# Other places for the half stores of a matmul with rotary embedding in ScalarE's program

## The chip, the cores and the metric

The kernel runs on one core of a Trainium2 chip. The metric is the device time of one execution in microseconds (us), as the median of several runs. A profile of one execution is at hand, with its trace.

Words used below: TensorE (PE in the profile) multiplies, VectorE (DVE) and ScalarE (ACT) read its results from PSUM, GpSimd (POOL) adds, SyncE (SP) issues loads. A line that ends in q (ACTq, SPq) is an issue of a DMA on that engine's queue.

## The reference

```python
y = np.matmul(x, weight)                       # x [16, 512, 768], weight [768, 768], float32
y = y.reshape(batch, seq, n_heads, head_dim)   # 12 heads of 64
y1, y2 = y[..., :32], y[..., 32:]
out1 = y1 * cos1 - y2 * sin1
out2 = y2 * cos2 + y1 * sin2
out = np.concatenate([out1, out2], axis=-1).reshape(batch, seq, hidden)
```

The 8192 rows of x are multiplied by one weight matrix, and each head of the result is rotated by tables that depend on the position in the sequence.

## The kernel before, in words

**Tiles, groups, pairs.** The rows make 64 tiles of 128 rows, numbered i. Four tiles make a group g (0 to 15); group g holds four batches at one of four position offsets, so that it needs one row of the tables. A group has two pairs, of two tiles each. A pair is plain or a block pair (the dictionary BLOCKS, L140 to L147). Twelve pairs are block pairs: the second pairs of groups 3 to 13 and of group 15. The other 40 tiles are plain.

**A plain tile.** SP loads it as float32 (`load`, 384 KB, ten buffers xs). ScalarE casts it to float16 (`castx`, xc<-xs). TensorE transposes it into PSUM (`turn_rows`, pt<-ident,xc, twelve half-height transposes that fill both pt banks). ScalarE copies it out (xt<-pt). The next tile's transposes need both banks again, so they wait for this copy. TensorE then multiplies it with the weights (py<-w_sb,xt).

**A block pair.** Both tiles are loaded in four quarters (`load_quarter`) that are arranged so that VectorE's 32x32 transpose finishes the job (xp). Seven pairs are loaded by SP as float32 (three buffers xb, quarters of 192 KB) and cast by ScalarE (`cast_pair`, xd<-xb, 1.6 us each). Five (groups 4, 6, 8, 10 and 12) are loaded by GpSimd with a cast on the way (xh, 96 KB each).

**After the product.** VectorE multiplies PSUM with the cos and sin tables (`rope`, L423), and GpSimd adds the two products into a group's output buffer (ov, L449), half a group (1536 columns) at a time up to group 11, in smaller pieces after that. There are four output buffers, so a group's sums wait for the stores of the group four before it. A store moves half a group, 768 KB (`store`, L481).

**Order of the work.** Every engine executes its program in the order in which the Python code emits it, and waits on semaphores in that order. The main loop (L686 to L724) runs over tiles i from 4 on. In one turn it emits: TensorE's matmuls of tile i (`both`), among them the transposes of a later plain tile and ScalarE's copy of it (`turns`, three tiles ahead); VectorE's transposes of block pairs (`bturns`); a further copy; ScalarE's casts of tiles five ahead or so, at most one in an even turn and two in an odd one (`casts`), and with each cast the load that may use the freed buffer (`pump`); GpSimd's loads; and last the stores that the dictionary `stores` has for this i (L718, L719).

Loads are issued by SP in a list made beforehand (`fetch`). Each load waits until the fifth load before it has landed, and until its buffer has been cast.

**Where the stores stand.** L651 to L664 fill `stores`. For each group but the last, and for its first half (h = 0) and second half (h = 2), it names the turn i in which the store is emitted, and the queue: ScalarE's up to group 12, SP's for groups 13 and 14. A store on ScalarE's queue waits for GpSimd's sum, and what stands behind it in ScalarE's program waits with it. A store that is emitted behind a cast cannot be issued before that cast's load has landed. The last group is stored in pieces at the end.

Between them ScalarE's casts and copies go in tile order. In the middle of the kernel a group has two casts and two copies of plain tiles, and, in every second group, the cast of a block pair between the two copies.

Of the kernel before, what the change touches and what calls it, by code (L numbers as in the profile page):

```python
# [108 lines left out]
def kernel(  # L109
# [23 lines left out]
    QB = 4  # L133
# [3 lines left out]
    LAST = NG - 1  # L137
# [514 lines left out]
    for g in range(LAST):  # L652
        for h in (0, 2):
            i = QB * (g + 1) + h
            q = (g, h * H, (h + 2) * H, "act")
            if g < 3:
                i += g + 1
            elif g < LAST - 4:
                i += QB + (1 if g in (3, LAST - 5) else 2)
            elif g < LAST - 2:  # L660
                i = QB * (LAST - 2) + 2 * (g - LAST + 4) + h // 2
            else:
                q = q[:3] + ("sp",)
            stores.setdefault(i, []).append(q)  # L664
# [21 lines left out]
    for i in range(QB, NTILE):  # L686
        g, s = divmod(i, QB)
# [81 lines left out]
```

## Time and profile before

| | |
|---|---|
| runs, median (lowest to highest) | 151.53 us (151.34 to 152.36), 3 runs |
| the profiled execution's own time | 151.91 us |
| its span, first to last instruction | 150.1 us |
| busy: TensorE, VectorE, ScalarE, GpSimd | 140.4, 127.8, 75.4, 124.0 us |
| DMA: moved, mean rate | 51.27 MB, 342 GB/s |
| ScalarE's half stores, issue to landing | 26, median 9.0 us |
| loads xs, issue to landing | 40, median 9.6 us |
| mean granted TensorE clock | 0.992 |

A row of the timeline has the start in us, the time in us, the engine, the line, the operation with its output and input tiles, and in brackets the idle time before it and what ended that. A row of a DMA queue has the number of packets, the MB and the time that its packets took as a share of 16 DMA engines; the shares of several queues can add to more than 100%. Queue q10 holds ScalarE's stores, q1 SP's loads (and SP's few stores at the end), q0 GpSimd's loads.

### The profile page before, as it was taken

What the parts mean: (1) busy time and instruction counts of PE and PEld (TensorE: products, weight loads), DVE (VectorE), ACT (ScalarE), POOL (GpSimd) and SP (SyncE); (2) the same over time, 40 slices, a digit from 0 to 9 for tenths busy, and PEclk for the clock granted to TensorE, in tenths of its full rate; (3) what the DMA queues carried; (4) which work ended last, traced back from release to release, by engine and by line L of the source; (5) the groups of instructions that cost most, each with busy time, mean ns of one, the idle gap of its engine ahead of it and who ended that gap; (6) DMA issues with size and microseconds to landing.
All of it is one profiled execution on the core that took longest, in us unless ns stands there. A gap on an engine that the chain in (4) does not pass through costs nothing.

```text
span 150.1 us, 4344 instructions
## 1 busy us (share of the span) xinstructions
PE 140.4 (94%) x1900; PEld 115.4 (77%) x1900; DVE 127.8 (85%) x101; ACT 75.4 (50%) x87; POOL 124.0 (83%) x77
## 2 busy tenths in 40 slices
PE   6769999999999999999999999999999996999970
PEld 2335578888888879999999999999999995765850
DVE  0334999888989998999989998999899996999990
ACT  3444798785443655375263734292536547930000
POOL 2000399999999999999999999598999997699990
PEclk9999999999999999999999999999999999999996
DMA  4999999999999999999999999999999999997574
GB/s 133 331 384 403 404 400 269 313 308 329 341 347 391 289 327 293 378 345 254 347 375 378 341 342 358 367 402 331 395 376 402 389 412 411 412 405 316 221 295 147
DMA packets 29155, 51.27 MB, mean 342 GB/s; under 512 B 7248, under 2 KB 15184, under 8 KB 29136
## 3 DMA queue, kind: packets, MB, share of 16 engines
q1 hardware_dynamic: 16336, 28.05, 55.0%
q10 hardware_dynamic: 7360, 20.97, 35.6%
q0 software_dynamic: 5440, 1.97, 11.2%
q8 instruction: 15, 0.25, 0.6%
q14 instruction: 4, 0.03, 0.1%
HBM read 27.79 MB, written 25.17 MB: 353 GB/s over the span
## 4 chain that ended last, share of the span: by engine, by line
DMA 74%; DVE 12%; SPq 6%; ACT 3%; issue 3%; DVEq 0%
DMA xs<-in_x_dram 51%; DMA xb<-in_x_dram 22%; DVE tq L423 8%; DVE w_raw L423 2%; SPq L236 2%; SPq L214 2%; ACT xd L194 1%; ACT xc L194 1%; ACT xt L194 1%; SPq L229 1%; DVE ov L449 1%; DVE xs L423 1%; SPq L501 0%; SPq L503 0%; SPq L534 0%
## 5 line engine op out<-in xcount | busy, mean ns | idle before, releaser
L449 POOL TENSOR_TENSOR ov<-tq 128x512 f32<-128x512 f32 (+3 forms) x35 | 76.7, 2221 | 20.8 <-DVE tq L423 20.6
L423 DVE TENSOR_TENSOR tq<-py,csn 128x1024 f32<-128x1024 f32 (+2 forms) x51 | 74.3, 1494 | 3.9 <-PE py L366 3.0
L366 PE MATMUL py<-w_sb,xt 64*128 64x512 f16 (+1 forms) x768 | 74.4, 323 | 0.0
L366 PEld LDWEIGHTS py<-w_sb,xt 64*128 64x128 f16 x768 | 55.7, 94 | 8.6 <-DVE tq L423 0.7
L366 PE MATMUL py<-w_sb,xp 64*128 64x256 f16 (+1 forms) x528 | 52.6, 323 | 0.0
L194 ACT COPY xt<-pt 128x768 f16<-128x768 f16 x38 | 30.4, 801 | 34.6 <-PE pt L275 30.5
L194 ACT CAST xc<-xs 128x768 f16<-128x768 f32 x40 | 36.0, 907 | 22.3 <-DMA xs<-in_x_dram 22.3
L366 PEld LDWEIGHTS py<-w_sb,xp 64*128 64x128 f16 x528 | 39.7, 94 | 4.3
L423 DVE TENSOR_TENSOR w_raw<-py,csn 128x1024 f32<-128x1024 f32 (+1 forms) x22 | 35.3, 1603 | 2.8 <-PE py L366 2.4
L449 POOL TENSOR_TENSOR ov<-w_raw 128x1536 f32<-128x1536 f32 (+2 forms) x15 | 35.4, 2380 | 0.5 <-DVE w_raw L423 0.4
L341 PE MATMUL py<-w_sb,xt 128*128 128x256 f16 (+1 forms) x102 | 17.0, 317 | 1.4 <-DVE w_sb L194 1.3
L275 PEld LDWEIGHTS pt<-ident,xc 64*128 64x128 f16 x408 | 13.4, 94 | 2.7 <-ACT xt L194 1.6
L275 PE MATMUL pt<-ident,xc 64*128 64x64 f16 x408 | 14.1, 190 | 1.3 <-ACT xt L194 1.3
L341 PEld LDWEIGHTS py<-w_sb,xt 128*128 128x128 f16 x102 | 9.2, 98 | 7.5 <-DVE w_sb L194 2.8
L194 ACT CAST xd<-xb 128x1536 f16<-128x1536 f32 x7 | 11.4, 1633 | 2.6 <-DMA xb<-in_x_dram 2.6
L229 POOL DMA_DIRECT2D xh<-in_x_dram x20 | 11.7, 590 | 0.0
L303 DVE STREAM_TRANSPOSE xp<-xd 128x768 f32<-128x768 f32 x7 | 6.8, 970 | 1.4 <-ACT xd L194 1.4
L194 DVE CAST w_sb<-w_raw 128x768 f16<-128x768 f32 x6 | 3.4, 558 | 4.2 <-DMA w_raw<-in_weight_dram 4.2
L303 DVE STREAM_TRANSPOSE xp<-xh 128x768 f32<-128x768 f32 x5 | 6.2, 1235 | 0.0
L558 PE MATMUL py<-cold 128*128 128x512 f16 x12 | 4.3, 519 | 1.4 <-DVE cold L486 1.4
L194 ACT COPY ov<-py 128x256 f32<-128x256 f32 x1 | 0.4, 372 | 10.1 <-POOL ov L449 10.1
L194 DVE COPY xt<-pt 128x768 f16<-128x768 f16 x2 | 1.1, 558 | 4.9 <-PE pt L260 4.9
(23 smaller groups left out, 22.6 us busy)
## 6 DMA issues: line engine op xcount, KB each, us to landing
out_dram<-ov ACTq DMA_DIRECT2D x26, 768.0 KB, 9.0
xs<-in_x_dram SPq DMA_DIRECT2D x40, 384.0 KB, 9.6
xb<-in_x_dram SPq DMA_DIRECT2D x28, 192.0 KB, 8.9
out_dram<-ov SPq DMA_DIRECT2D x4, 768.0 KB, 4.8
w_raw<-in_weight_dram SPq DMA_DIRECT2D x6, 384.0 KB, 7.5
xh<-in_x_dram POOLq DMA_DIRECT2D x20, 96.0 KB, 8.0
out_dram<-ov SPq DMA_DIRECT2D x1, 384.0 KB, 3.7
out_dram<-ov ACTq DMA_DIRECT2D x1, 384.0 KB, 3.4
```

What stands on the lines that cost most here:

```text
L194: eng.copy(out=o, in_=i_) if e == "act" else eng.tensor_copy(out=o, in_=i_)
L214: do(e, lambda eng: eng.dma_start(out=xs_b[k], in_=x[b].rearrange("(p r) h -> r p h", r=SB)[r]), writes=[f"xs{k}"], dma=f"xs{k}")
L229: do(e, lambda eng: eng.dma_start(out=dst[ts(q, R)], in_=src[r, q]), writes=[f"{name}q{q}"], dma=name)
L236: do(e, lambda eng: eng.dma_start(out=w_raw[:, t, h], in_=wv[t, h]), writes=[f"wr{t}{h}"], dma=f"ov{t}_{1536 * (1 - h)}")
L275: do("pe", lambda eng: eng.transpose(pts[r][:, t, h, :], src[rows, t, h, :], ident[rows, rows]), reads=[f"xc{c}", "ident"], writes=[f"pt{r ...
L303: do("dve", lambda eng: eng.transpose(out=dst, in_=src), reads=rd, writes=[f"xp{z}"])
L341: do("pe", lambda eng: eng.matmul(ps, get(t, h), w_sb[:, t, h, a - s * H : z - s * H], start=start, stop=stop), reads=[key, f"w{t}{h}"], w ...
L366: do("pe", lambda eng: eng.matmul(py[:, a:z], get(t, h)[rows], w_sb[rows, t, h, a - s * H : z - s * H], start=start, stop=not opens and en ...
L423: do("dve", lambda eng: eng.tensor_tensor(out=tq.rearrange("p j (h d) -> p j h d", d=D), in0=ps.rearrange("p (h d) -> p h d", d=D) .unsque ...
L449: do(adder, lambda eng: eng.tensor_tensor(out=ov_b[o][:, ds(c0, w)].rearrange("p (h t d) -> p h t d", t=2, d=HD), in0=tq[:, 0].rearrange(" ...
L558: do("pe", lambda eng: eng.matmul(py[:, ts(b, 512)], cold[:, 0:P], cold, start=True, stop=warmed[0] < WARM - 6), reads=["cold"], writes=[f ...
```

## The change

Only the turns i in which ScalarE's stores up to group 12 are emitted are changed. SP's stores of groups 13 and 14, and everything else, stand as before. TensorE's, VectorE's, GpSimd's and SP's programs are the same; in ScalarE's program the same 26 half stores stand at other places.

```diff
-            if g < 3:
-                i += g + 1
-            elif g < LAST - 4:
-                i += QB + (1 if g in (3, LAST - 5) else 2)
-            elif g < LAST - 2:
-                i = QB * (LAST - 2) + 2 * (g - LAST + 4) + h // 2
+            if g < LAST - 2:
+                i = (((5, 7), (9, 12), (15, 16))[g] if g < 3 else (QB * g + 6, QB * g + 9))[h // 2]
             else:
                 q = q[:3] + ("sp",)
```

Here QB is 4, LAST is 15, and before these lines i is 4 (g + 1) + h. The turns that come of it, for the first and the second half of a group:

| group | before | after |
|---|---|---|
| 0 | 5, 7 | 5, 7 |
| 1 | 10, 12 | 9, 12 |
| 2 | 15, 17 | 15, 16 |
| 3 | 21, 23 | 18, 21 |
| 4 to 9 | 4g + 10, 4g + 12 | 4g + 6, 4g + 9 |
| 10 | 49, 51 | 46, 49 |
| 11 | 52, 53 | 50, 53 |
| 12 | 54, 55 | 54, 57 |

In ScalarE's program this puts a store behind each copy of a plain pair. Around the stores of group 8 the program reads as follows, in order. Before: copy 45, store of group 8's first half, cast 48, cast 49, store of its second half, copy 48, copy 49, store of group 9's first half. After: copy 41, store of group 8's first half, cast 44, cast 45, copy 44, cast of a block pair, store of group 8's second half, copy 45, store of group 9's first half, cast 48, cast 49, copy 48, store of group 9's second half, copy 49, store of group 10's first half. Where a pair's cast stands between two copies (groups with an odd number, 3 to 13), the store that follows it stands behind that cast.

## The prediction

> **What bounds the kernel now.** I read the page first, then TensorE's timeline, ScalarE's timeline, GpSimd's timeline, and the DMA view over short stretches. On the page, TensorE and the DMA engines are both full nearly to the end, and the chain of waits is 74% DMA:
>
> ```profile
> PE 140.4 (94%) x1900; PEld 115.4 (77%) x1900; DVE 127.8 (85%) x101; ACT 75.4 (50%) x87; POOL 124.0 (83%) x77
> ...
> PE   6769999999999999999999999999999996999970
> ...
> DMA  4999999999999999999999999999999999997574
> ...
> DMA 74%; DVE 12%; SPq 6%; ACT 3%; issue 3%; DVEq 0%
> ```
>
> TensorE's timeline decides what can be won. In the table of stretches it is busy without a gap from 18 to 124 us. The only gap after that and before its last instruction at 145.4 is this one:
>
> ```profile
> 123.82 2.11 PE L366 MATMUL py<-w_sb,xp 64*128 64x512 f16 x24
> 127.23 0.35 PE L275 MATMUL pt<-ident,xc 64*128 64x64 f16 x12 [1.29 <-ACT xt L194]
> ```
>
> Its cause stands in ScalarE's timeline. The cast of the last block pair (xd<-xb) waits for its DMA until 124.89, the copy of tile 57 (xt<-pt, 126.37) stands behind that cast, and TensorE's transposes of tile 58 need the PSUM banks that this copy reads:
>
> ```profile
> 122.61 0.91 ACT L194 CAST xc<-xs 128x768 f16<-128x768 f32 x1
> 124.89 1.59 ACT L194 CAST xd<-xb 128x1536 f16<-128x1536 f32 x1 [1.37 <-DMA xb<-in_x_dram]
> 126.37 0.80 ACT L194 COPY xt<-pt 128x768 f16<-128x768 f16 x1
> ```
>
> So at most 1.3 us can be won. What can be lost depends on the loads' slack, smallest at tile 49, whose cast waits for its load until 103.55:
>
> ```profile
> 103.55 0.91 ACT L194 CAST xc<-xs 128x768 f16<-128x768 f32 x1 [2.24 <-DMA xs<-in_x_dram]
> 103.56 0.43 ACTq L481 DMA_DIRECT2D out_dram<-ov  x1
> 105.61 0.80 ACT L194 COPY xt<-pt 128x768 f16<-128x768 f16 x1 [1.15 <-PE pt L275]
> 107.73 0.80 ACT L194 COPY xt<-pt 128x768 f16<-128x768 f16 x1 [1.32 <-PE pt L275]
> ```
>
> TensorE's transposes of tile 49 begin at 107.25. A later load pushes cast 49 (0.91) and behind it the copy of tile 48 (0.80), which frees the banks; the slack is 107.25 - 103.55 - 0.91 - 0.80 = 2.0 us. The second line matters too: the store (second half of group 8) issues just as the load lands, because it stands behind that cast. In the kernel before, second halves of groups 4 to 8 wait behind a late load and so give way to it.
>
> The DMA view shows ScalarE's store ring (q10) beside the loads (q1) and GpSimd's casting loads (q0), first over 67.6 to 71.2, then over 71.2 to 113, then over 118 to 130:
>
> ```profile
> q1 hardware_dynamic: 473, 0.68, 71.0%
> q0 software_dynamic: 647, 0.23, 53.9%
> q10 hardware_dynamic: 1, 0.00, 0.0%
> ```
>
> ```profile
> q10 hardware_dynamic: 2982, 8.64, 53.2%
> q1 hardware_dynamic: 4395, 6.05, 44.3%
> q0 software_dynamic: 1238, 0.45, 8.6%
> ```
>
> ```profile
> DMA packets 1931, 4.92 MB, mean 410 GB/s; under 512 B 138, under 2 KB 399, under 8 KB 1930
> ...
> q10 hardware_dynamic: 1176, 3.41, 70.8%
> q1 hardware_dynamic: 754, 1.50, 32.1%
> ```
>
> Where the store ring is empty the loads have 71% of the engines; where it is full, 44% and less. By the packet records the ring is empty from 50.8 to 53.3, 58.9 to 59.9 and 67.6 to 71.2, and then full, but for 0.3 us, to 135.8.
>
> **The change part by part.** No instruction, byte or buffer is added; stores move in ScalarE's program alone.
>
> Issue times. In the new order a store issues when TensorE hands over the transposes of the copy before it. From those copies: group 2's second half 50.41 to 47.3 (behind tile 21's cast); group 3's 56.72 to 50.5 and 58.84 to 56.7; first halves of groups 4 to 9 some 8 us sooner (group 8: 99.59 to 91.4), second halves 3 to 6 us (103.56 to 97.5); group 10 107.7 and 113.8 for 113.77 and 115.89; group 11 115.9 for 118.19, its second half unchanged.
>
> Their own wait, for GpSimd's sum. Behind a waiting store stand the next copy and casts, and TensorE waits for these. Group 10's first sum ends at 101.06 + 3.46 = 104.5, and its store now issues at 107.7: 3.2 us to spare. The other moved stores have 2.8 us or more, group 1's first half 1.2 (sum done 30.9, copy at 32.05). Cost 0; it would show if GpSimd fell 1.2 to 3 us behind. An issue takes 0.4 us of the sequencer before and after.
>
> Buffers. GpSimd's sums wait for stores four groups back; these have landed some 9 us before they are needed (group 4's first at 76.1, group 8's sum starts at 85.2), so sooner brings nothing: 0.
>
> Price of a half store: 786,432 bytes at the 410 GB/s of 118 to 130 is 1.92 us of all engines.
>
> How far the stores run ahead. The holes at 51, 59 and 68 us get filled. At 103.5 the ring before has finished group 7 and a quarter of group 8's first half (102.65 to 106.54). After, group 8's second half issues at 97.5, starts 3 us later (the row at 99.59 starts at 102.65), takes 4 us, and is three quarters done: 1.5 half stores ahead, 2.9 us of all engines. At 44.3% of the engines the loads are then 2.9 / 0.443 = 6.5 us late. The slack is 2.0, so 4.5 us are missing at tile 49.
>
> What TensorE waits. While it waits, sums and stores stop too and the loads get all engines, 1 / 0.443 = 2.26 us of progress per us: 4.5 / 2.26 = 2.0 us. It comes in pieces of up to 1 us from tile 25 on (slack 1.8), since each wait moves all later needs. Bounds: 0, if filling the holes is free, and 4.5, if the stores in flight keep their share all the while. I take 2.0: in the new ring a store starts 3 us after its issue and finds the one before it all but done, so it soon runs dry.
>
> [...] The row is 2,982 packets of q10 beside 4,395 of q1, the latter partly 768-byte ones, and 53 to 44% in time. [...]
>
> The gap at 127.2. At 124.86, when the last pair lands now, the ring has served half of group 11's first half (123.12 to 126.56); after, with everything 2.0 us later, it has served 0.8 to 1.0 of it, and the next store waits behind tile 58's cast as before. 0.3 to 0.5 half stores more is 0.6 to 1.0 us; I take 0.8. The pair lands at 125.7 and TensorE resumes at 128.0. Being 2.0 late it gets there at 125.94 + 2.0 = 127.9: of the gap of 1.29 only 0.1 is left, and what follows is 0.8 us later.
>
> Group 12's second half moves back, 128.33 to 131.9. It is done by 140 either way, the last store lands at 148.9, and the ring stands idle from 135.8 to 144.5, which is its cover: 0.
>
> Sum: +2.0 - 1.2 = +0.8 us. The profiled execution took 151.91 us (span 150.1 and 1.8 around it), 0.38 above the median 151.53. So 152.7 for it, 152.3 for the median.
>
> **Rivals.**
> Loads starve deeper: the backlog of stores keeps its share while TensorE waits. For it: stores no longer stand behind late casts, and one is nearly always in service. Against: the new ring is limited by its issues from about 100 us on. Wait 2.8 (from where it decides) to 4.5, less the gap of 1.29: +1.5 to +3.2, some 154.0.
>
> The holes are free (the other side). For it: at 50.8 to 53.3 and 67.6 to 71.2 the engines moved only 228 and 255 GB/s. If a store raised that to 410, (410 - 245) x 6.1 us is 1.0 MB or 1.3 half stores for nothing; the lead left is 0.2 stores, 0.9 us of load time, under the slack of 2.0. The last pair lands over 1 us sooner and the gap closes: -1.3, 150.2. It decides once 1.0 half stores are free (the 0.5 left are 2.2 us, about the slack). Against: the queues' shares there add to 125% and 154%, so engines were taken, by small packets.
>
> The clock. TensorE's granted clock is 1.00 in the stretch with the 1.29 us gap, and 0.53 over 147.5 to 150, some 2.1 us after its last instruction. A single wait beyond 2.1 us could therefore halve it; first matmuls at 1.40 and the full clock on record from 4.28 put the loss at half of 2.9, 1.4 us each time. One drop on top of 2.8 us of waiting: +2.9, 154.4. Against: the waits should come in pieces under 1 us. [...]
>
> No effect: the ring serves the stores in the old rhythm, 151.5.
>
> **How the numbers follow.** Forecast 0.48, starving deeper 0.33, free holes 0.10, clock 0.06, no effect 0.03. Faster by over 1% (under 150.0, about what a measurement of this kernel can tell from no change) needs more than the whole gap: half of the free holes' chance, 0.05. Slower by over 1% (over 153.05): deeper starving, the clock and 0.04 of the forecast's upper end, 0.43. The rest, 0.52, is within. Forecast's own range 151.5 to 153.2. The range runs from the free holes, rounded up for a part of them, 150.4, to the wait of 4.5: 151.53 + 3.2, with 0.3 for the 0.38 between executions, 155.0.
>
> **What would show it.** Right: store issues right after copies, no ScalarE wait for GpSimd in the middle; q10 busy at 51 to 53 and 68 to 71; casts waiting longer for xs and xb between 70 and 105; TensorE gaps summing to 2 us there, released by ScalarE casts or copies; the gap near 127 nearly gone. Wrong: no TensorE gap before 120, or one store wait on GpSimd that holds a copy, or gaps over 2 us at one place.

## The result and the profile after

| | kernel before | changed kernel |
|---|---|---|
| runs on the same chip, median (lowest to highest), us | 151.95 (149.65 to 155.84), 22 runs | 153.05 (151.38 to 155.74), 22 runs |
| ratio of the times, with its 95% interval | 1 | 1.0135 [1.0098, 1.0171] |
| a profiled execution's own time (span), us | 151.91 (150.1) | 153.1 (151.2) |
| a second profiled execution (run e1 below) | 150.38 (148.6) | |

Executions more than 1.5% above the fastest of their kernel (11 of the 22 before, 5 of the 22 after) are left out of the ratios but not of the medians, which are 0.7% apart; by that rule e5 has no ratio, and as its profile and those of e2 and e3 are of such executions, no size of a difference is rested on them.

The change made the kernel 1.35% slower, about 2.0 us of 151. The page of the changed kernel has the same busy times, but the chain of waits names other things. Of 74% DMA in the profile before, 17% is left, and TensorE stands first:

```profile
PE 141.4 (93%) x1900; PEld 112.8 (75%) x1900; DVE 128.1 (85%) x101; ACT 75.4 (50%) x87; POOL 124.1 (82%) x77
...
PE 54%; DMA 17%; DVE 14%; issue 3%; SPq 3%; POOL 2%; ACT 2%; ACTq 0%; DVEq 0%; POOLq 0%
```

That is no gain: the shares tell through which instructions one path from the end runs, not whether it became shorter. What TensorE lost is told by its timeline. From 18 us to its last matmul it now has two gaps (stretches without a matmul). First the one in the middle:

```profile
101.64 0.38 PE L366 MATMUL py<-w_sb,xt 64*128 64x512 f16 x1
102.81 3.51 PE L366 MATMUL py<-w_sb,xt 64*128 64x512 f16 x40 [0.79 <-ACT xt L194]
```

and then the one near the end, over a shorter window of the same timeline:

```profile
128.15 0.35 PE L275 MATMUL pt<-ident,xc 64*128 64x64 f16 x12 [1.18 <-ACT xt L194]
```

Together they are 0.79 + 1.18 = 1.97 us, which is 1.3% of 151. Both are of one execution. The second one stands where the profile before had 1.29 us. ScalarE's timeline of the changed kernel gives the cause of the first:

```profile
96.85 0.91 ACT L194 CAST xc<-xs 128x768 f16<-128x768 f32 x1 [3.84 <-DMA xs<-in_x_dram]
97.67 0.79 ACT L194 COPY xt<-pt 128x768 f16<-128x768 f16 x1
100.35 1.61 ACT L194 CAST xd<-xb 128x1536 f16<-128x1536 f32 x1 [1.88 <-DMA xb<-in_x_dram]
100.35 0.90 ACTq L481 DMA_DIRECT2D out_dram<-ov  x2
101.85 0.81 ACT L194 COPY xt<-pt 128x768 f16<-128x768 f16 x1
```

The cast of group 11's block pair (xd<-xb) waits 1.88 us for its load. Tile 45's copy stands behind it and runs at 101.85; TensorE's matmuls of tile 45 resume at 102.81. The store line carries two issues: the second half of group 8 and the first half of group 9 both waited behind that cast. In the kernel before the same stretch has no wait of the pair's cast, because its load landed at 95.89 and not at 100.32:

```profile
97.46 0.80 ACT L194 COPY xt<-pt 128x768 f16<-128x768 f16 x1 [2.09 <-PE pt L275]
98.16 1.66 ACT L194 CAST xd<-xb 128x1536 f16<-128x1536 f32 x1
99.59 0.38 ACTq L481 DMA_DIRECT2D out_dram<-ov  x1
99.69 0.82 ACT L194 COPY xt<-pt 128x768 f16<-128x768 f16 x1
```

The list of ScalarE's waits sums this up (us in total, times, longest). After:

```profile
ACT xc L194 <- DMA xs<-in_x_dram: 32.7, 16, 4.1
ACT xd L194 <- DMA xb<-in_x_dram: 4.4, 4, 1.9
```

Before:

```profile
ACT xc L194 <- DMA xs<-in_x_dram: 22.3, 14, 3.4
ACT xd L194 <- DMA xb<-in_x_dram: 2.6, 2, 1.4
```

Most of the 10.4 us more on the first line are hidden: those casts run ahead of what TensorE needs. In e1, the same program as before, the first line has 15.8 us, so single executions differ here too. The DMA view of the changed kernel shows where the loads' time went. Over 50.8 to 53.3 us, where the store ring was empty before:

```profile
DMA packets 545, 0.89 MB, mean 355 GB/s; under 512 B 209, under 2 KB 304, under 8 KB 545
...
q10 hardware_dynamic: 205, 0.62, 63.7%
q1 hardware_dynamic: 144, 0.19, 24.7%
```

The stores took this hole, and the loads' share fell (before: 50.3%). The engines moved 355 GB/s there instead of 228. But GpSimd's casting loads (q0) also had fewer packets in it, 196 for 697, so a part of that rise is small packets that came at another time. Over 71.2 to 113 the shares are about those of before:

```profile
q10 hardware_dynamic: 2809, 8.14, 50.2%
q1 hardware_dynamic: 4311, 6.10, 44.4%
```

The packet records give the stores' lead. Half stores served (q10), and MB moved by all other queues, nearly all of it loads, up to a time:

| up to, us | 60 | 75 | 90 | 103.5 | 124.9 |
|---|---|---|---|---|---|
| half stores: before | 6.00 | 9.09 | 12.82 | 16.08 | 22.48 |
| half stores: e1, the same program | 6.04 | 9.27 | 12.81 | 16.26 | 22.35 |
| half stores: after | 7.00 | 10.55 | 14.04 | 17.75 | 22.95 |
| loads, MB: before | 15.06 | 17.58 | 20.05 | 22.43 | 25.78 |
| loads, MB: e1 | 15.07 | 17.66 | 20.23 | 22.60 | 25.98 |
| loads, MB: after | 14.77 | 17.17 | 19.74 | 21.73 | 25.37 |

At 103.5 us the stores lead those of the first profile by 1.67 half stores (1.31 MB), and the loads are behind by 0.70 MB. Against e1 the lead is 1.49 (1.17 MB) and the loads are behind by 0.87 MB.

Two kernels further below, e10 and e12, also run the program of the kernel before until past 106 us, where their first moved store stands. So four executions of one program can be set beside the changed kernel at 103.5 us:

| | before | e1 | e10 | e12 | after |
|---|---|---|---|---|---|
| half stores served | 16.08 | 16.26 | 16.62 | 16.81 | 17.75 |
| loads moved, MB | 22.43 | 22.60 | 22.76 | 21.84 | 21.73 |
| all queues, MB | 35.08 | 35.39 | 35.83 | 35.05 | 35.70 |
| group 11's pair landed at, us | 95.89 | 95.31 | 94.39 | 99.19 | 100.32 |

The stores' lead is clear of this spread, with 0.94 half stores against e12, and so is the pair's landing, by 1.1 us (100.50 in e7 and 100.54 in e9, which have the same stores of groups 4 to 9). What all engines moved is not: the 0.61 MB that the lead exceeds the loads' deficit by (0.30 against e1) is no more than executions of one program differ by.

### The profile page after: what moved, and what is told of

The parts are those of the page before. It is cut to its first block, busy times and chain, and to the rows that moved or that the text cites. A ratio compares the mean times of both kernels' runs of the same rounds, so it can differ in the third digit from the quotient of the medians.

```text
span 151.2 us, 4345 instructions
## 1 busy us (share of the span) xinstructions
PE 141.4 (93%) x1900; PEld 112.8 (75%) x1900; DVE 128.1 (85%) x101; ACT 75.4 (50%) x87; POOL 124.1 (82%) x77
## 3 DMA queue, kind: packets, MB, share of 16 engines
q0 software_dynamic: 5440, 1.97, 10.9%
## 4 chain that ended last, share of the span: by engine, by line
PE 54%; DMA 17%; DVE 14%; issue 3%; SPq 3%; POOL 2%; ACT 2%; ACTq 0%; DVEq 0%; POOLq 0%
PE py L366 46%; DVE tq L423 10%; DMA xb<-in_x_dram 7%; DMA xs<-in_x_dram 6%; DMA w_raw<-in_weight_dram 5%; PE py L341 4%; PE pt L275 3%; DVE w_raw L423 2%; POOL ov L449 2%; SPq L214 2%; ACT xd L194 1%; SPq L229 1%; DVE xp L303 1%; PE pt L260 1%; DVE ov L449 1%
## 5 line engine op out<-in xcount | busy, mean ns | idle before, releaser
L366 PEld LDWEIGHTS py<-w_sb,xt 64*128 64x128 f16 x768 | 53.8, 94 | 11.5 <-DVE tq L423 1.5
L366 PEld LDWEIGHTS py<-w_sb,xp 64*128 64x128 f16 x528 | 38.5, 94 | 5.3
L558 PE MATMUL py<-cold 128*128 128x512 f16 x12 | 4.8, 568 | 1.4 <-DVE cold L486 1.4
```

Of the source, the lines that this page charges most:

```text
L366: do("pe", lambda eng: eng.matmul(py[:, a:z], get(t, h)[rows], w_sb[rows, t, h, a - s * H : z - s * H], start=start, stop=not opens and en ...
L558: do("pe", lambda eng: eng.matmul(py[:, ts(b, 512)], cold[:, 0:P], cold, start=True, stop=warmed[0] < WARM - 6), reads=["cold"], writes=[f ...
```

## The experiments

The theory is that of the prediction: bytes of stores that go out sooner take the shared DMA engines from the loads, and TensorE loses only what the lateness has beyond the slack. Rival A, the lost brake: it is the second halves alone, which no longer stand behind a late cast. Rival B, the program: it is the places of the stores in ScalarE's program, whatever bytes they carry. Rival C, the window: SP has too few loads in flight (`AHEAD`, each load waits for the fifth before it) to catch up.

All runs are kernels with the turns as a table, `i = PLACES[g][h // 2]`, one pair (first half, second half) per group 0 to 12; the diffs show the rows that differ. Each ratio is against the kernel before in the same session.

**e1: the kernel before, once more**

```diff
-                i = (((5, 7), (9, 12), (15, 16))[g] if g < 3 else (QB * g + 6, QB * g + 9))[h // 2]
+                i = PLACES[g][h // 2]
+    PLACES = ((5, 7), (10, 12), (15, 17), (21, 23), (26, 28), (30, 32), (34, 36), (38, 40), (42, 44), (46, 48), (49, 51), (52, 53), (54, 55))
```

> The kernel before once more, with the places of the stores written as a table. It shows what the comparison says of no change, and whether TensorE's gap near 127 us stands in a second profile. Theory (stores ahead of loads on the shared DMA engines): ratio 1.000 within 0.006, no TensorE gap between 18 and 124 us, one gap of 0.5 to 1.5 us near 127 behind the last block pair's cast. Rival (the profiles differ by chance and the change has no place of its own): gaps at other places, of 1 us or more, in this profile too.

Measured: 0.9994 [0.9950, 1.0038], no difference from the same program. Its profile is the surprise: 150.38 us, and no gap of TensorE from 18 us to the end. The line at the place of the 1.29 us gap, and ScalarE's cast that leads to it:

```profile
125.69 0.35 PE L275 MATMUL pt<-ident,xc 64*128 64x64 f16 x12
```

```profile
123.31 1.63 ACT L194 CAST xd<-xb 128x1536 f16<-128x1536 f32 x1
124.83 0.81 ACT L194 COPY xt<-pt 128x768 f16<-128x768 f16 x1
```

The last pair landed at 122.30 here and at 124.86 in the first profile; the cast has no bracket, so it waited for nothing. The same program has the gap in one execution and not in the other.

**e2: only the first halves moved; e3: only the second halves moved**

```diff
 e2: first halves as after, second halves as before
+    PLACES = ((5, 7), (9, 12), (15, 17), (18, 23), (22, 28), (26, 32), (30, 36), (34, 40), (38, 44), (42, 48), (46, 51), (50, 53), (54, 55))
 e3: second halves as after, first halves as before
+    PLACES = ((5, 7), (10, 12), (15, 16), (21, 21), (26, 25), (30, 29), (34, 33), (38, 37), (42, 41), (46, 45), (49, 49), (52, 53), (54, 57))
```

> First halves at the new places, second halves at the old ones. Theory (lead of the stores): some 1.0 half store of lead at 103 us, loads some 4 us later there, casts waiting longer than before; TensorE gaps of 0 to 1 us in the middle; ratio 1.000 to 1.007. Rival A (the lost brake: only the second halves matter, since in the kernel before they stand behind casts that wait for loads): ratio 1.000, no gap in the middle. Rival B (places in ScalarE's program: each store behind a copy holds up what TensorE waits for): about half of the change's 1.35%, 1.007, with ScalarE waiting for GpSimd.

> Second halves at the new places, first halves at the old ones. Theory (lead): some 0.5 half store of lead on average, gaps of 0 to 0.5 us in the middle, ratio 1.000 to 1.005. Rival A (lost brake): nearly all of the change, 1.010 or more, with TensorE gaps between 70 and 110 us. Rival B (places in ScalarE's program): about 1.007.

Measured: e2 1.0056 [1.0011, 1.0102], e3 0.9990 [0.9937, 1.0042]. The second halves alone cost nothing that can be seen, so rival A falls. The first halves alone cost 0.56% by the ratio, where the whole costs 1.35%, but the interval reaches to 1.02%.

**e4: the changed kernel with the lead taken out in bytes**

```diff
+        if (g, c0) in ((3, 0), (3, 2 * H), (4, 0)):
+            c1 = c0 + H
```

> The changed kernel, all stores at their new places, but the two halves of group 3 and the first half of group 4 store only half of their bytes (the second of the two batches of each is left out of the output): 1.5 half stores, 1.18 MB, as much as the lead was reckoned to be. Theory (lead on the DMA engines): 2.9 us of all engines come free before 70 us, no TensorE gap between 18 and 124 us, the gap near 127 shrinks under 0.5 us or goes, ratio to the kernel before 0.988 to 0.997. Rival B (places in ScalarE's program): the places are those of the changed kernel, so 1.010 to 1.017 as there.

Measured: 0.9994 [0.9956, 1.0032]; profile 150.58 us, no gap of TensorE from 18 us on. All places are those of the change, and its loss is gone with 1.18 MB less of stores, 1.5 half stores. By 103.5 us 16.43 half stores were served, close to the 16.26 of e1. The pair's cast that waited 1.88 us in the changed kernel:

```profile
98.69 1.64 ACT L194 CAST xd<-xb 128x1536 f16<-128x1536 f32 x1 [0.50 <-DMA xb<-in_x_dram]
98.70 1.21 ACTq L483 DMA_DIRECT2D out_dram<-ov  x2
100.23 0.79 ACT L194 COPY xt<-pt 128x768 f16<-128x768 f16 x1
```

Rival B falls. The pair landed at 98.67, within the spread of the kernel before's own program. The theory had expected less than 1, because it still held that a gap of 1.29 us was there to be won. The kernel before with the same bytes left out was not run; e1 says that it would have no gap to win.

**e5: the kernel before with the lead put in as bytes**

```diff
+        if i in (18, 22):
+            extra(*((2 * H, 12) if i == 18 else (H, 14)))
 ... (left out here: the definition of extra, and group 14's wait for it)
```

`extra` issues one more transfer on ScalarE's queue, 768 KB and then 384 KB out of the weights' buffer, to rows that group 14's stores overwrite later; the stores stand where they stood before.

> The kernel before with all its stores at their old places, and two more DMAs on ScalarE's queue: 768 KB behind the casts of turn 18 and 384 KB in turn 22, from the weights to rows of the output that group 14's stores write later (these wait for them). They add 1.18 MB of stores at about 50 and 59 us, as much as the lead that was reckoned, wait for nothing on GpSimd and are waited for by none before 132 us. Theory (lead of the stores on the shared DMA engines): casts wait longer for loads (30 us or more in sum where the kernel before had 15.8 in its second profile and 22.3 in its first), TensorE gaps of 1 to 3 us in sum, most near 100 and near 127; ratio 1.010 to 1.025. Rival B (places of the stores in ScalarE's program): the places are old, ratio 1.000 to 1.003.

Measured: median 156.08 us (153.3 to 156.55, six runs), 151.76 for the kernel before in that session; no ratio. All six took 153.3 us or more, and 5 of the 30 of the kernel before did. The trace has gaps at the same two stretches. The first stands behind the cast of a plain tile whose load was late, the second behind the last pair's cast:

```profile
98.61 0.89 ACT L194 CAST xc<-xs 128x768 f16<-128x768 f32 x1 [4.31 <-DMA xs<-in_x_dram]
100.25 0.35 PE L275 MATMUL pt<-ident,xc 64*128 64x64 f16 x12 [1.44 <-ACT xt L194]
127.72 1.54 ACT L194 CAST xd<-xb 128x1536 f16<-128x1536 f32 x1 [1.33 <-DMA xb<-in_x_dram]
130.01 0.50 PE L275 MATMUL pt<-ident,xc 64*128 64x64 f16 x12 [3.01 <-ACT xt L194]
```

Bytes alone, at unmoved places, go with longer times here, as the theory has it and rival B has not. That they made these gaps isn't shown: e3, whose ratio is 1, has gaps of 0.28 and 2.54 us in its traced execution too.

**e7, e8, e10: only the middle, only the early, only the last groups moved**

```diff
 e7: groups 4 to 9 as after, the rest as before
+    PLACES = ((5, 7), (10, 12), (15, 17), (21, 23), (22, 25), (26, 29), (30, 33), (34, 37), (38, 41), (42, 45), (49, 51), (52, 53), (54, 55))
 e8: groups 1 to 3 as after, the rest as before
+    PLACES = ((5, 7), (9, 12), (15, 16), (18, 21), (26, 28), (30, 32), (34, 36), (38, 40), (42, 44), (46, 48), (49, 51), (52, 53), (54, 55))
 e10: groups 10 to 12 as after, the rest as before
+    PLACES = ((5, 7), (10, 12), (15, 17), (21, 23), (26, 28), (30, 32), (34, 36), (38, 40), (42, 44), (46, 48), (46, 49), (50, 53), (54, 57))
```

> Only the stores of groups 4 to 9 at the new places. Theory (lead): the lead is there from 60 to 105 us, and is given back by 115 when groups 10 and 11 come at the old places; TensorE gap near 102 of 0.3 to 1 us, little near 127; ratio 1.003 to 1.010.

> Only the stores of groups 1 to 3 at the new places. Theory (lead): the holes of the store ring at 51 and 59 us are filled, the hole at 68 us becomes longer and gives the lead back; no TensorE gap near 102; ratio 0.998 to 1.003. If the early filling alone were what costs, 1.007 or more.

> Only the stores of groups 10 to 12 at the new places. Theory (lead): nothing changes before 105 us, so no TensorE gap near 102; some 0.5 half store more is stored by 125 us, the last block pair lands up to 1 us later, a gap of 0 to 1.5 us near 127 in the profile; ratio 1.000 to 1.006.

Measured: e7 1.0069 [1.0033, 1.0105], e8 1.0047 [0.9988, 1.0106], e10 0.9961 [0.9912, 1.0010]. In e8's trace are gaps of 0.39 us at 58.26 and 1.69 at 127.45, in e10's none. e7's trace has one gap. It is as long as the changed kernel's and lies in the same stretch, but it stands behind another cast: that of tile 45, a plain tile, and the copy after it. The cast of group 11's pair begins only after it:

```profile
98.36 0.91 ACT L194 CAST xc<-xs 128x768 f16<-128x768 f32 x1 [3.91 <-DMA xs<-in_x_dram]
99.17 0.79 ACT L194 COPY xt<-pt 128x768 f16<-128x768 f16 x1
100.01 0.35 PE L275 MATMUL pt<-ident,xc 64*128 64x64 f16 x12 [0.80 <-ACT xt L194]
100.52 1.61 ACT L194 CAST xd<-xb 128x1536 f16<-128x1536 f32 x1 [0.56 <-DMA xb<-in_x_dram]
```

So the stores of groups 4 to 9 alone bring a loss of this size in the middle; which late load makes it differs from execution to execution. e8 and e10 are not told from no change. The three parts add up to 0.69 + 0.47 - 0.39 = 0.77%, the whole is 1.35%; their intervals allow it, and so does a slack that a part stays under and the whole does not.

**e9: the changed kernel with seven loads ahead**

```diff
-    AHEAD = 5
+    AHEAD = 7
```

> The changed kernel with seven loads allowed in flight in place of five (AHEAD = 7). Theory (lead: the loads are short of a share of the DMA engines, and their queue is never empty): deeper in flight brings no share, the casts wait about as long, TensorE gaps near 102 and 127 stay; ratio to the kernel before 1.008 to 1.017, as for the change. Rival C (the loads are late since too few are in flight when stores take turns with them): gaps gone, ratio 0.998 to 1.003.

Measured: 1.0127 [1.0040, 1.0214], no better than the changed kernel; gaps of 0.89, 0.40 and 2.15 us, the middle ones at 83 and 87 us, and 36.4 us of waiting for xs. The loads were in flight longer (xs: median 12.6 us from issue to landing, 9.3 in the changed kernel) and were not cast sooner. Rival C falls: the loads lack engines, not permission.

**e6, e11, e12: stores later than before**

```diff
 e6: groups 3 to 9 two turns later, the last groups later too
+    PLACES = ((5, 7), (10, 12), (15, 17), (24, 26), (28, 30), (32, 34), (36, 38), (40, 42), (44, 46), (48, 50), (52, 53), (54, 55), (58, 59))
 e11: groups 3 to 9 two turns later (group 3's first half three)
+    PLACES = ((5, 7), (10, 12), (15, 17), (24, 26), (28, 30), (32, 34), (36, 38), (40, 42), (44, 46), (48, 50), (51, 52), (53, 54), (55, 57))
 e12: only groups 10 to 12 later, by one or two turns
+    PLACES = ((5, 7), (10, 12), (15, 17), (21, 23), (26, 28), (30, 32), (34, 36), (38, 40), (42, 44), (46, 48), (50, 52), (53, 54), (55, 57))
```

> Stores the other way: groups 3 to 9 two turns later than in the kernel before, group 10 at 52 and 53, group 11 at 54 and 55, group 12 at 58 and 59. Theory (lead): the loads run ahead, casts wait under 15 us in sum for xs, no TensorE gap between 18 and 130 us; ratio 0.992 to 1.000, and fewer executions over 151.5 us than the kernel before has. Rival B: the stores stand elsewhere but not behind copies of plain pairs, 1.000. It would be slower if GpSimd's sums had to wait for a buffer.

> Groups 3 to 9 two turns later than in the kernel before, as in the run with all stores later; group 10 at 51 and 52, group 11 at 53 and 54, group 12 at 55 and 57, so that about one half store less is left for the end than there. Theory (lead): no TensorE gap between 18 and 130 us, and the end is no longer bound by stores that are left over; ratio 0.990 to 1.000, and a spread as small as in the run with all stores later.

> Groups 3 to 9 as in the kernel before, groups 10 to 12 at 50 and 52, 53 and 54, 55 and 57. Theory (lead): about one half store less by 125 us than before, so that the last block pair lands up to 2 us sooner; no gap near 127; nothing else changes; ratio 0.992 to 1.000.

Measured: e6 1.0034 [1.0000, 1.0067], e11 1.0038 [1.0000, 1.0076], e12 0.9960 [0.9918, 1.0001]. In e6 TensorE has no gap from 18 us on, and yet nothing is won: the stores that were held back are now left over at the end. The table of stretches (PE, PEld, DVE, ACT and POOL busy, clock, DMA share, GB/s) of e6:

```profile
132.00:140.00 8.00, 8.00 (x72) 5.73 (x69) 7.83 (x9) 0.80 (x1) 8.00 (x8) 1.00 1.02 402
140.00:148.00 8.00, 4.04 (x39) 3.35 (x36) 4.92 (x9) 0.37 (x1) 4.78 (x5) 0.89 0.88 336
```

and of e1, the kernel before:

```profile
132.00:140.00 8.00, 8.00 (x72) 5.82 (x71) 7.83 (x9) 0.80 (x1) 8.00 (x8) 1.00 0.86 341
140.00:148.00 8.00, 3.90 (x38) 3.22 (x35) 4.80 (x9) 0.37 (x1) 4.66 (x5) 0.87 0.71 261
```

With the engines fuller to the end (1.02 and 0.88 for 0.86 and 0.71), e6's last store lands 3.63 us after its issue (145.18 to 148.81), e1's 2.30 us after (145.06 to 147.36). e11, which expected a gain, missed it; its only gap is 0.17 us, and what the rest of its 0.4% is stays open. e12 is the best kernel of the study by its ratio, but its interval touches no change, so it is no proven gain. Its 12 runs lie within 149.64 to 150.91 us, those of the kernel before in that session within 149.67 to 155.55.

## Why the prediction was right or wrong

**The direction and the mechanism were right, the places and sizes of the waits were not.** The changed kernel is slower, and e4 shows that the loss goes with the stores' bytes. The size was too small: within 1% was given the most chance, and the loss is 1.35%. The lead was reckoned as 1.5 half stores at 103.5 us and measured as 1.67 (0.94 to 1.67 over the four executions). Casts waited longer between 70 and 105, and ScalarE released the gaps, as written. The other signs did not come: the gaps in the middle sum to 0.79 us and not to 2, and the gap near 127 is not nearly gone. Of the store ring's three holes one was filled; the others were at 58.30 to 60.62, longer than before, and at 68.21 to 69.79, and new ones were at 45.23 to 46.17 and 83.79 to 85.70.

**The failing step is the sum's term of -1.2 for the gap at 127.** It took a gap of 1.29 us, seen in one profiled execution of 151.91 us, as a part of the kernel before that a delay could be laid over. The second profile (e1, 150.38 us) has none, and 151.91 is 1.5% above the fastest of the 22 runs, 149.65. Where no gap is, nothing can be laid over it, and the changed kernel's whole 1.97 us is lost. Without the credit the prediction's own sum would have been +2.0, the measured loss. That agreement is luck, since the loss is divided otherwise in the traced execution: 0.79 in the middle and 1.18 at 127. Even against the execution with the gap the term failed: 0.1 us was to be left of it, and 1.18 us are there. The last pair landed at 125.78, as the 125.7 reckoned, but TensorE reached the spot only 1.0 us later than before (1.03 from 125.94 to 126.97, where its 1.18 us begin), not 2.0 later.

**The middle wait was over-sized: 2.0 reckoned, 0.79 measured.** The loads were to be 6.5 us late at tile 49. Measured, tile 45's load was late by 2.4 us (cast at 96.85 for 94.46), group 11's pair by 4.4 and tile 49 by 0.2 (cast at 103.76 for 103.55). The wait came behind the pair's cast at 100.35. A pair's load had no slack reckoned at all. It was 3.6 us: landed 0.79 us sooner than at 100.32, at 99.53, the load would have cost nothing, and before it landed at 95.89. The executions agree with that limit: the pair landed at 98.67 in e4 and at 99.19 in e12, without a gap of TensorE there (0.1 us at most). They also show that not all of the 4.4 us is the change's: the kernel before's own program landed the pair anywhere from 94.39 to 99.19. Why the loads were less late than 6.5 us stays open. That a part of the stores' bytes went beside the loads, as the rival of the free holes has it, is not clear of the spread at 103.5 us.

**The issue times were right for the first halves, not for the second.** Group 8's first half issued at 91.42 (91.4 reckoned), its second at 100.35 (97.5). The second half's store of an even group stands behind the cast of the next group's block pair, so a late load still holds it. The prediction read a store as issued with the copy before it and overlooked the cast between, which the description of the change names; a part of the old brake was left. What that was worth was not measured.

**Costs put at 0 held.** ScalarE's copies were not held by GpSimd: the one wait put down to it (1.3 us at 108.77) is as long as the 1.32 us that the same copy waited for TensorE before, and TensorE has no gap there. No sum waited longer for its buffer.

**The rivals.** Starving deeper (+1.5 to +3.2) holds the measured total, but not by its mechanism: it wanted 2.8 us or more in the middle. The clock had no part: the granted clock stays at 1.00 around both gaps. The limit of 2.1 us that the prediction took for a single wait does not hold either; the last section has the traces on it. The free holes needed 1.0 half stores for nothing; whatever was free was not enough, as the gap near 127 did not close. No effect is out.

What stays open: why two executions of one program differ by 2.6 us in when the last pair lands, and four by 4.8 us in when group 11's does; and 0.5 us of the way from e1 to the changed kernel. TensorE's last row of matmuls starts at 142.82 in e1 and at 145.28 after, 2.46 later, and the gaps are 1.97 of it.

## What to carry to other kernels

Take a second profile of the kernel before, and compare the profiled time with the fastest runs, before a gap in it is put into a sum: a gap that only one execution has can't be won back, and can't cover a delay. Where stores and loads share the engines, compare the lead of stores that go out sooner with the slack of every kind of load, the large ones behind which copies stand first, and take that slack from the latest landing in several executions: one program's landings can differ by as much as the change moves them (here by 4.8 us, where the changed kernel's pair landed 4.4 later than that of the first profile). Landings within the slack cost nothing here (98.67 us in e4 and 99.19 in e12, with gaps of at most 0.1 us); if one a little beyond it costs only the excess, parts of a change needn't add up.

## What the runs showed of the hardware

The length of a gap alone does not decide whether TensorE's granted clock falls. It stayed at 1.00 after gaps of 2.04 us (e2), 2.15 (e9) and 2.54 (e3). It was halved after e5's gap of 3.01 us, but also within 1.96 us of the last matmul in e1 (143.90 to 145.86); in the changed kernel 2.79 us after it (146.36 to 149.15). The prediction had put the limit at 2.1 us by the first profile, where it fell 2.20 us after the last matmul (145.44 to 147.64). After the gap in e5 it stayed halved for 3.41 us (129.96 to 133.37 by the clock's records); the table of stretches of e5 has it in the last column but two:

```profile
126.00:130.00 4.00, 1.00 (x14) 0.64 (x10) 0.91 (x2) 2.67 (x4) 1.91 (x2) 0.99 1.03 416
130.00:132.00 2.00, 1.99 (x22) 1.19 (x24) 2.00 (x3) 2.00 (x3) 0.48 (x1) 0.50 1.03 418
132.00:134.00 2.00, 2.00 (x29) 1.24 (x27) 1.64 (x2) 0.26 (x1) 2.00 (x3) 0.66 1.04 418
134.00:138.00 4.00, 4.00 (x56) 2.67 (x49) 2.69 (x3) 2.39 (x3) 2.57 (x4) 1.00 1.02 405
```

What decides beside the length of the gap was not shown.

While GpSimd's casting loads were moved in small packets (in the kernel before 697 packets with 0.25 MB over 50.8 to 53.3 us, where 716 of all 944 packets were under 512 bytes), earlier stores went with more bytes moved in these runs. Up to 60 us the three kernels with all of the early stores of groups 1 to 3 moved 20.17 to 20.28 MB (the changed kernel, e8 and e9), and the four executions of the kernel before's program 19.72 to 20.08. The room is 0.1 to 0.6 MB of the 0.79 MB that the stores led by, and the queues' shares, which over 50.8 to 53.3 us add to more than 100% with the stores (112% in the changed kernel) and without (157% in the kernel before), do not tell of it.
